# Value and gate projection of a gated linear recurrence: high and low weight parts as one 512-column product, and the output projection's first rows in two rounds

## The chip, the core and the metric

The kernel runs on one core of a Trainium2 chip. A core has a matrix engine (TensorE, written PE in the profile; its weight loads are the row PEld), a vector engine (VectorE, DVE), an engine for pointwise functions (ScalarE, ACT), a general one (GpSimd, POOL) and SyncE (SP), whose queue issues nearly all of this kernel's transfers. Each engine works through its own list of instructions in order and waits on semaphores that the other engines raise. PE reads its operands from the on-chip memory SBUF and writes only to the accumulator memory PSUM, which ACT and DVE read. The metric is the device time of the core in microseconds (us), before against after.

## The reference, cut to what matters

The model is a trunk of two layers over 1024 tokens of width 1024. The first layer mixes tokens with a gated linear recurrence in 8 heads of 128 columns, the second with windowed attention; each mixer is followed by a layer norm, a gated feed-forward with a short convolution (the ConvFFN), and another layer norm. The change lies in the first mixer:

```python
q, f, i, g = jnp.split(h @ w_in, 4, axis=-1)
fg = lb + (1.0 - lb) * jax.nn.sigmoid(heads(f))
o = hgrn2_chunkwise(jax.nn.silu(heads(q)), 1.0 - fg, heads(i), jnp.log(fg))
o = o * lax.rsqrt(jnp.mean(jnp.square(o), -1, keepdims=True) + RMS_EPS)
o = o * g_norm_w.astype(jnp.float32) * jax.nn.silu(heads(g))
return o.reshape(B, S, D).astype(h.dtype) @ w_out
```

Here `i` are the values (V in the kernel) and `silu(g)` is the output gate (G). The state of a head is a 128 x 128 matrix that decays with `fg` and takes in a key times a value at every token. All of it is float32.

## The kernel before, in words

**Three products for one.** Each float32 operand is split into a high part (a rounded copy in the type fp32r, made by ACT) and a low part (the remainder, a subtraction on DVE in `low_part`, L169). A product is then hi x hi + hi x lo + lo x hi, three matmuls that accumulate in the same PSUM columns: lines L194, L195 and L196 of `mm3`. `T[:, 0]` and `T[:, 1]` hold the high and low parts of the transposed activations, `HL` those of the weights.

**Stages of the first mixer.** For each head h the order is: `qf` projects forget gate and query (weights stationary, 512 tokens moving, four products of 24 matmuls), then `ig_block` is called four times, for pairs tp of token blocks, and projects value and gate: the 128 x 128 activations of one token block are stationary and 256 weight columns move, 128 of the value and 128 of the gate. A pair of blocks fills one PSUM tile `psmm` of 512 columns. There are four tiles `psmm`, used in turn by everything that is projected. From each, ACT takes the sigmoid of the gate (L706) and copies the value (L707), and DVE multiplies the gate by its sigmoid (L709); after that the tile is free. The very first pair of head 0 is projected by `first_rows` (L688) in an order of its own, while the input is still arriving.

**The recurrence.** `recur` of head h runs between the matmuls of the projections that follow. It is a chain over engines: DVE scales keys and queries level by level (`update`), ACT makes copies (`stash`), PE multiplies small blocks (`scores`, `blocks`), and so on to the products kd x V (L1020) and the output (L1034, L1036). Then `norm` squares on ACT, scales on DVE (L1055), and PE transposes (L1060). For head 7 the transposed output is split straight into `T` (L225, L226); the other heads' outputs wait in `Y`, and `moves` splits them into `T` later, in head 7, two token blocks at a time.

**What sets the order.** Within the first mixer the order of all engines but the transfers' landing is written out by hand with the help of a planner, the class `Order`: `od.t` is planned PE time, moved on by the cost of each matmul; `od.v` is planned DVE time; `od.tick()` after a product lets chains step whose time has come, and `lay` fills DVE with waiting work: low parts of weights (`lowparts`), low parts of moved activations (`movelows`), and block differences of the feed-forward's weights (`pending`, L1134), which have nothing to do with this layer. `slot_begin` and `slot_end` bracket each product or pair of blocks; at `slot_begin` all low parts of the slot before, and all waiting gate multiplications (`soon`), are given out at once. Past the first mixer only PE's order is written out, and the other engines' order comes from a scheduler.

**The output projection.** Its first six row blocks are begun with seven of eight contraction blocks (`out_part`), since head 7's output comes last: blocks 0 to 3 in `psmm`, 4 and 5 in the halves of a tile `psax`. `out_proj` then adds the eighth, loads the residual into `Y` (L305) and the second half of the weights (`out_late`, by way of L164), and the layer norm follows.

Of the kernel before, what the change touches and what calls it, by code (L numbers as in the profile page):

```python
# [16 lines left out]
P = 128  # L17
# [90 lines left out]
def trunk(ctx: ExitStack, tc: tile.TileContext, a: dict, out: bass.AP):  # L108
# [31 lines left out]
    def psmm():  # L140
        return mmp.tile([P, 512], F32, name="psmm")
# [57 lines left out]
    def mm32(ps, lhsT, rhs, start=True, stop=True, cost=0.218, **kw):  # L199
        nc.tensor.matmul(ps, lhsT, rhs, start=start, stop=stop, **kw)  # L200
        od.t += cost
# [451 lines left out]
    with tc.tile_pool(name="t", bufs=1, reuse_waits="tile") as raws, hgrn_pool as hp:  # L653
# [27 lines left out]
        def first_rows(us, ps, ahead):  # L681

            for i in range(2):
                passes = [(0, 0, 0), (1, 0, 0), (0, 0, 1), (1, 0, 1), (0, 1, 0), (0, 1, 1)] if i == 0 else [
                    (0, 0, 0), (0, 0, 1), (0, 1, 0), (0, 1, 1), (1, 0, 0), (1, 0, 1)]
                for n, (x, w, u) in enumerate(passes):
# [6 lines left out]
                    od.tick()  # L693

        def ig_block(h, us, tp, soon=None, ahead=None):
            if tp == 0:
                VG[h] = (hp.tile([P, NB, P], F32, name="V", bufs=2), hp.tile([P, NB, P], F32, name="G", bufs=2))
            V, G = VG[h]
            ps = psmm()
# [4 lines left out]
            pv = ps.rearrange("p (t g c) -> p t g c", t=2, g=2)  # L704
            ts = slice(2 * tp, 2 * tp + 2)
            nc.scalar.activation(G[:, ts, :], pv[:, :, 1, :], AF.Sigmoid)  # L706
            nc.scalar.copy(V[:, ts, :], pv[:, :, 0, :])  # L707
            def gate():
                nc.vector.tensor_tensor(G[:, ts, :], G[:, ts, :], pv[:, :, 1, :], op=ALU.mult)  # L709
                od.vec(0.4)  # L710

            if soon is None:
                gate()
            else:
                soon.append(od.later(1.2, gate))

# [11 lines left out]
        with tc.tile_pool(name="ep", bufs=1, reuse_waits="tile") as ep:  # L728
# [22 lines left out]
            with tc.manual_schedule(engines={EN.PE, EN.SP, EN.Activation, EN.DVE}):  # L751
# [52 lines left out]
                for tp in range(1, NB // 2 - 1):  # L804
                    ahead = od.spawn(x_pair(2 * tp + 2), 2.0)
                    ig_block(0, us, tp)
                    od.finish([ahead])
                w0["f"] = qf_split(raws0["f"])
                ig_block(0, us, NB // 2 - 1)
                w0["q"] = qf_split(raws0["q"])  # L810
                nc.vector.tensor_copy(msk, mf)

# [61 lines left out]
        def recur(h, qs, fg, kp):  # L874
# [82 lines left out]
            od.vec(4.4)  # L957
            idle = [t.rearrange("p c d -> p (c d)") for t in VG[h - 1]]
            r1 = idle[1][:, :S // 2]
            nc.vector.tensor_tensor(r1, kp[:, 0::2], qp[:, 1::2], op=ALU.mult)  # L960
# [6 lines left out]
            update(1)  # L967
            early = stash(2, idle[0])
            yield od.behind(0.0, 0.5)
# [44 lines left out]
            while values_in[0] < h:  # L1014
                yield 0.2
            V, G = VG[h]
            ps = psax()
# [57 lines left out]
        slot_no = [-1]  # L1075
        pending, soon, lowparts, movelows = [], [], [], []

# [67 lines left out]
        values_in, values_done, normed = [0], [-1], []  # L1145
        wo = a["hgrn_w_out"][0]
# [7 lines left out]
        with tc.manual_schedule(engines={EN.PE, EN.SP, EN.Activation, EN.DVE, EN.Pool}):  # L1154
# [23 lines left out]
            for h in range(1, NH):  # L1178
# [18 lines left out]
                for tp in range(NB // 2):  # L1197
                    if tp == lead[h]:
                        ready.append((h, w["out"]))
                    slot_begin()  # L1200
                    if h == NH - 1 and tp:
                        moved.append(od.spawn(moves(tp - 1), 0.8))
                        if tp == 1:
                            oraw.append(load(out_loads(rows1, 0, (6, 7))))
                    ig_block(h, us, tp, soon)
                    slot_end(2.0, *make_w[tp])
                values_in[0] = h
                if ready:
# [4 lines left out]
            while lowparts:  # L1213
                lay_low()
            od.finish([params] + moved[:2] + soon)
# [346 lines left out]
```

## Time and profile before

| | us |
|---|---|
| median of 3 runs (lowest, highest) | 2152.23 (2151.32, 2153.89) |
| the profiled execution: its own time | 2151.58 |
| its span, from first to last instruction | 2149.8 |
| PE busy | 2135.9 (99%) |
| DVE busy | 1743.3 (81%) |
| ACT busy | 918.5 (43%) |
| POOL busy | 122.1 (6%) |

The page of the profile gives busy time by engine, the span in 40 slices, the transfers, the chain of work that ended last, and the costliest groups of instructions. Other views give the same trace as stretches of time, as waits, or as a list in order of time. A row of a group reads: line, engine, operation, output<-input, shapes, count | busy time, mean nanoseconds of one | idle time before it and who ended it. Matmuls overlap in the pipeline: the duration of one (0.39 us for 512 columns) is longer than the distance from one start to the next, and only that distance is what a matmul costs PE.

### The profile page before, as it was taken

How to read it: one execution, taken by the hardware profiler on the slowest of the kernel's cores; microseconds unless marked ns; L12 is line 12 of the kernel's file. 1: busy time of each engine (PE TensorE's matmuls, PEld its weight loads, DVE VectorE, ACT ScalarE, POOL GpSimd, SP SyncE). 2: the span in 40 equal slices, each digit the busy share in tenths (PEclk: the TensorE clock that was granted, in tenths of full speed). 3: DMA queues.
4: the chain of work that ended last, by engine and by line, in shares of the span. 5: the costliest groups of instructions: out<-in, count | busy, mean ns of one | idle time of the engine just before them, and what ended most of it. 6: DMA issues, size and time to landing. Idle time of an engine off the chain costs nothing.

```text
span 2149.8 us, 33060 instructions
## 1 busy us (share of the span) xinstructions
PE 2135.9 (99%) x13165; PEld 1809.0 (84%) x13165; DVE 1743.3 (81%) x2318; ACT 918.5 (43%) x1472; POOL 122.1 (6%) x143
## 2 busy tenths in 40 slices
PE   9999999999999999999999999999999999999998
PEld 9899999898888888888888888878888888888887
DVE  3877765577999999887978558969999899878986
ACT  3344434353444444434433256743544444444430
POOL 1000000001100000000001123311000000000002
PEclk9999999999999999999999999999999999999999
DMA  5755541123222222228854411133233222249662
GB/s 200 292 204 211 177 138 41 34 85 123 99 85 95 86 89 81 82 93 284 279 186 157 128 30 30 33 118 108 89 98 98 85 82 89 79 144 329 226 213 92
DMA packets 229842, 279.03 MB, mean 130 GB/s; under 512 B 29960, under 2 KB 158648, under 8 KB 226872
## 3 DMA queue, kind: packets, MB, share of 16 engines
q1 hardware_dynamic: 228736, 276.53, 38.5%
q8 instruction: 103, 1.69, 0.3%
q10 hardware_dynamic: 856, 0.37, 0.1%
q14 instruction: 51, 0.42, 0.1%
q0 software_dynamic: 96, 0.02, 0.0%
HBM read 213.94 MB, written 62.94 MB: 129 GB/s over the span
## 4 chain that ended last, share of the span: by engine, by line
PE 96%; DVE 2%; DMA 1%; issue 0%; ACT 0%; SPq 0%; DVEq 0%; ACTq 0%
PE psmm L194 20%; PE psmm L196 20%; PE psmm L195 20%; PE psax L194 9%; PE psax L196 9%; PE psax L195 9%; PE psax L200 3%; PE psmm L204 1%; PE psmm L200 1%; PE psax L204 1%; PE psax L1356 1%; DMA rx<-in_ffn_w_out_dram 1%; DVE T L169 0%; DVE Y L473 0%; PE psmm L688 0%
## 5 line engine op out<-in xcount | busy, mean ns | idle before, releaser
L194 PE MATMUL psmm<-T,HL 128*128 128x512 f32 x768 | 305.0, 397 | 0.0
L196 PE MATMUL psmm<-T,HL 128*128 128x512 f32 x768 | 299.4, 390 | 0.0
L195 PE MATMUL psmm<-T,HL 128*128 128x512 f32 x768 | 299.1, 389 | 0.0
L473 DVE SCALAR_TENSOR_TENSOR Y<-Y,cwt 128x1023 f32<-128x1023 f32 (+1 forms) x176 | 225.1, 1281 | 41.1 <-ACT Y L471 39.5
L221 ACT CAST HL<-rx 128x1024 fp32r<-128x1024 f32 (+1 forms) x151 | 152.0, 1009 | 200.8 <-PE psmm L195 46.9
L194 PE MATMUL psmm<-HL,T 128*128 128x256 f32 (+1 forms) x640 | 192.3, 300 | 0.9 <-issue 0.9
L196 PE MATMUL psmm<-HL,T 128*128 128x256 f32 (+1 forms) x640 | 189.8, 297 | 0.0
L195 PE MATMUL psmm<-HL,T 128*128 128x256 f32 (+1 forms) x640 | 189.6, 296 | 0.0
L169 DVE TENSOR_TENSOR HL<-rx,HL 128x1024 fp32r<-128x1024 f32 (+1 forms) x151 | 174.6, 1162 | 11.0 <-ACT HL L221 10.7
L196 PEld LDWEIGHTS psmm<-T,HL 128*128 128x128 f32 x768 | 144.1, 188 | 30.9
L194 PEld LDWEIGHTS psmm<-T,HL 128*128 128x128 f32 x768 | 144.3, 188 | 28.6
L195 PEld LDWEIGHTS psmm<-T,HL 128*128 128x128 f32 x768 | 144.4, 188 | 27.9
L471 ACT ACTIVATE Y<-Y,cwt 128x1024 f32<-128x1024 f32 x88 | 109.0, 1239 | 99.3 <-DVE Y L460 90.5
L194 PE MATMUL psax<-T,HL 128*128 128x512 f32 x352 | 137.3, 390 | 0.0
L196 PE MATMUL psax<-T,HL 128*128 128x512 f32 x352 | 137.0, 389 | 0.0
L195 PE MATMUL psax<-T,HL 128*128 128x512 f32 x352 | 137.0, 389 | 0.0
L195 PEld LDWEIGHTS psmm<-HL,T 128*128 128x128 f32 x640 | 122.3, 191 | 4.2 <-issue 1.0
L243 POOL TENSOR_TENSOR rs<-rs,nhalf 128x1 f32<-128x1 f32 x32 | 46.2, 1445 | 1398.7 <-DVE rs L242 1398.7
L194 PEld LDWEIGHTS psmm<-HL,T 128*128 128x128 f32 x640 | 122.3, 191 | 3.7 <-issue 0.4
L196 PEld LDWEIGHTS psmm<-HL,T 128*128 128x128 f32 x640 | 122.2, 191 | 3.5 <-DVE T L169 0.3
L169 DVE TENSOR_TENSOR HL<-raw,HL 128x1024 fp32r<-128x1024 f32 x51 | 62.2, 1222 | 71.9 <-ACT HL L176 71.8
L221 ACT CAST HT<-rx 128x1024 fp32r<-128x1024 f32 (+1 forms) x37 | 35.6, 962 | 113.9 <-DVE rx L427 74.3
(302 smaller groups left out, 5117.7 us busy)
## 6 DMA issues: line engine op xcount, KB each, us to landing
rx<-in_ffn_w_in_dram SPq DMA_DIRECT2D x136, 256.0 KB, 3.1
rx<-gd SPq DMA_DIRECT2D x118, 256.0 KB, 3.8
Y<-in_ffn_w_out_dram SPq DMA_DIRECT2D x44, 512.0 KB, 5.7
bsd<-Y SPq DMA_DIRECT2D x22, 1024.0 KB, 5.2
gd<-Y SPq DMA_DIRECT2D x44, 512.0 KB, 2.6
rx<-in_ffn_w_out_dram SPq DMA_DIRECT2D x54, 256.0 KB, 4.3
R<-bsd SPq DMA_DIRECT2D x44, 256.0 KB, 5.0
Y<-in_ffn_w_in_dram SPq DMA_DIRECT2D x40, 256.0 KB, 3.1
```

Source lines behind the costliest of these rows:

```text
L169: make = lambda e: e.tensor_tensor(lo, src, hi.bitcast(F32), op=ALU.subtract)
L194: nc.tensor.matmul(ps, st(0), mv(0), start=start, stop=False)
L195: nc.tensor.matmul(ps, st(0), mv(1), start=False, stop=False)
L196: nc.tensor.matmul(ps, st(1), mv(0), start=False, stop=stop)
L200: nc.tensor.matmul(ps, lhsT, rhs, start=start, stop=stop, **kw)
L204: nc.tensor.transpose(ps, src, ident)
L221: nc.scalar.copy(hi, src)
L243: nc.gpsimd.tensor_tensor(rs, rs, nhalf, op=ALU.pow)
L471: nc.scalar.activation(c, u, AF.Identity, bias=cwt[:, l, 3, ci:ci + 1], scale=cwt[:, l, 2, ci:ci + 1])
L473: nc.vector.scalar_tensor_tensor(c[:, sh:], u[:, :S - sh], cwt[:, l, 2 - sh, ci:ci + 1], c[:, sh:], op0=ALU.mult, op1=ALU.add)
L1356: nc.tensor.matmul(pv[:, e, jj, lo:], q[bp // 2][es, e, qs], Kl[es, pp, ks] if low else Kh[:, pp, e, ks], start=not low and jj == 0, stop= ...
```

## The change

**Value and gate.** For every token block but the first two of head 0, the three matmuls of 256 columns become two. The first has the high part of the activations stationary and moves the high and the low part of the weights behind each other, 512 columns, into a whole tile `psmm`: columns 0 to 255 receive hi x hi, columns 256 to 511 receive hi x lo. The second has the low part of the activations stationary and adds lo x hi to the first 256 columns. The two halves still have to be added, so the new chain `values` takes the place of the sigmoid, copy and multiplication that read PSUM: ACT copies the right half to SBUF, DVE adds the left half, and after each second block ACT takes the sigmoid of the gates and DVE multiplies. Each token block now takes a tile `psmm` of its own. `V` and `G` become one tile `VG` with value and gate beside each other.

**Planner.** A contraction block of this projection is now booked with 0.347 us of planned PE time; it was 3 x 256 / 2365 = 0.325. Low parts and chains left over from one slot are given out at the end of the next slot (`rest`), not at its beginning.

**Output projection.** Blocks 0 to 3 are begun in two rounds: first all products of the high activations with both weight parts, for the four blocks, then the products of the low activations for the four blocks. The low parts of moved activations are asked for only ahead of the second round.

```diff
-        VG = {-1: tuple(hp.tile([P, NB, P], F32, name=n, bufs=2) for n in "VG")}
+        VG = {-1: hp.tile([P, NB, 2, P], F32, name="VG", bufs=2)}
+        def values(h, tb, ps):
+            vg = VG[h][:, tb]
+            nc.scalar.copy(vg, ps[:, 256:].rearrange("p (g c) -> p g c", g=2))
+            yield 0.9
+            nc.vector.tensor_tensor(vg, vg, ps[:, :256].rearrange("p (g c) -> p g c", g=2), op=ALU.add)
+            od.vec(0.45)
+            if tb == NB - 1:
+                values_in[0] = h
+            if tb % 2:
+                G = VG[h][:, tb - 1:tb + 1, 1, :]
+                sg = hp.tile([P, 2, P], F32, name="sg")
+                yield 0.7
+                nc.scalar.activation(sg, G, AF.Sigmoid)
+                yield 0.8
+                nc.vector.tensor_tensor(G, G, sg, op=ALU.mult)
+                od.vec(0.4)
...
+            for tb in () if ahead else (2 * tp, 2 * tp + 1):
+                ps, ts = psmm(), slice(tb * P, (tb + 1) * P)
+                for kc in range(KC):
+                    w = us[kc // 4]
+                    nc.tensor.matmul(ps, T[:, 0, kc, ts], w[:, :, kc % 4, :], start=kc == 0, stop=False)
+                    nc.tensor.matmul(ps[:, :256], T[:, 1, kc, ts], w[:, 0, kc % 4, :], start=False, stop=kc == KC - 1)
+                    od.t += 0.347
+                    od.tick()
+                soon.append(od.spawn(values(h, tb, ps)))
...
-            if ahead:
-                first_rows(us, ps, ahead)
-            else:
-                proj_tok(us, tp, ps)
-            nc.scalar.activation(G[:, ts, :], pv[:, :, 1, :], AF.Sigmoid)
-            nc.scalar.copy(V[:, ts, :], pv[:, :, 0, :])
-            def gate():
-                nc.vector.tensor_tensor(G[:, ts, :], G[:, ts, :], pv[:, :, 1, :], op=ALU.mult)
-                od.vec(0.4)
...
+            od.finish(gated[h])
             og = hp.tile([P, NB, P], F32, name="og")
...
-        def slot_begin():
+        def rest():
             while lowparts:
                 lay_low()
-            od.finish(soon)
-            soon.clear()
+            od.finish(old)
+            soon[:] = [t for t in soon if t[1] is not None]
+            old[:] = soon
...
         def slot_end(wait, *makes):
+            rest()
...
             for tb in range(4):
                 begun.append(psmm())
+                ts = slice(tb * P, (tb + 1) * P)
+                for w in range(2):
+                    for kc in range(KC - 1):
+                        nc.tensor.matmul(begun[tb], T[:, 0, kc, ts], us[kc][:, w, :], start=w + kc == 0, stop=False)
+                        od.t += 512 / 2365.0
+                        od.tick()
+            for tb in range(4):
+                ts = slice(tb * P, (tb + 1) * P)
                 movelows.sort(key=lambda m: m[0])
                 while movelows and movelows[0][0] <= tb // 2:
                     lay_moved()
-                out_part(begun[tb], us, tb, range(KC - 1))
+                for kc in range(KC - 1):
+                    nc.tensor.matmul(begun[tb], T[:, 1, kc, ts], us[kc][:, 0, :], start=False, stop=False)
+                    od.t += 512 / 2365.0
+                    od.tick()
```

More of the change, by code (lines that the diff above doesn't have):

```diff
@@ L669, in qf_split @@
             return split_raw(raw, eng).rearrange("p h (k c) -> p h k c", k=KC)
-        VG = {-1: tuple(hp.tile([P, NB, P], F32, name=n, bufs=2) for n in "VG")}
+        VG = {-1: hp.tile([P, NB, 2, P], F32, name="VG", bufs=2)}
+        values_in, soon, gated = [-1], [], {}
+        def values(h, tb, ps):
[14 more added lines that the diff above has]
+                od.vec(0.4)
@@ new lines, in first_values, with ig_block @@
+        def first_values(ps):
+            pv = ps.rearrange("p (t g c) -> p t g c", t=2, g=2)
+            vg = VG[0][:, :2]
+            nc.scalar.activation(vg[:, :, 1, :], pv[:, :, 1, :], AF.Sigmoid)
+            nc.scalar.copy(vg[:, :, 0, :], pv[:, :, 0, :])
+            yield 1.4
+            nc.vector.tensor_tensor(vg[:, :, 1, :], vg[:, :, 1, :], pv[:, :, 1, :], op=ALU.mult)
+            od.vec(0.4)
+        def ig_block(h, us, tp, ahead=None):
+            if tp == 0:
+                VG[h] = hp.tile([P, NB, 2, P], F32, name="VG", bufs=2)
+            if ahead:
+                ps = psmm()
+                first_rows(us, ps, ahead)
+                soon.append(od.spawn(first_values(ps)))
+                gated[h] = soon[-1:]
+            for tb in () if ahead else (2 * tp, 2 * tp + 1):
[7 more added lines that the diff above has]
+                soon.append(od.spawn(values(h, tb, ps)))
+                gated.setdefault(h, []).append(soon[-1])
+                od.tick()
@@ L673, in ig_first, with soon_all @@
+        def soon_all(left=0):
+            while len(soon) > left:
+                od.finish([soon.pop(0)])
         def ig_first(raw):
@@ L693, in first_rows @@
                     od.tick()
[L695 to L699, printed above, removed]
-            if ahead:
-                first_rows(us, ps, ahead)
-            else:
-                proj_tok(us, tp, ps)
[L704 to L707, printed above, removed]
-            def gate():
-                nc.vector.tensor_tensor(G[:, ts, :], G[:, ts, :], pv[:, :, 1, :], op=ALU.mult)
-                od.vec(0.4)
[L712 to L715, printed above, removed]
         still = Y[:, 7, :P]
@@ L807, in trunk @@
                     od.finish([ahead])
+                    soon_all(1)
                 w0["f"] = qf_split(raws0["f"])
@@ L957, in recur @@
             od.vec(4.4)
-            idle = [t.rearrange("p c d -> p (c d)") for t in VG[h - 1]]
-            r1 = idle[1][:, :S // 2]
+            idle = VG[h - 1].rearrange("p c g d -> p (c g d)")
+            r1 = idle[:, S:S + S // 2]
             nc.vector.tensor_tensor(r1, kp[:, 0::2], qp[:, 1::2], op=ALU.mult)
@@ L967, in recur @@
             update(1)
-            early = stash(2, idle[0])
+            early = stash(2, idle[:, :S])
             yield od.behind(0.0, 0.5)
@@ L1075, in trunk @@
         slot_no = [-1]
-        pending, soon, lowparts, movelows = [], [], [], []
+        pending, lowparts, movelows, old = [], [], [], []
         def lay_low():
@@ L1203, in trunk @@
                         if tp == 1:
+                            rest()
                             oraw.append(load(out_loads(rows1, 0, (6, 7))))
-                    ig_block(h, us, tp, soon)
+                    ig_block(h, us, tp)
                     slot_end(2.0, *make_w[tp])
-                values_in[0] = h
                 if ready:
@@ L1214, in trunk @@
                 lay_low()
-            od.finish([params] + moved[:2] + soon)
+            soon_all()
+            od.finish([params] + moved[:2])
             moved.append(od.spawn(moves(NB // 2 - 1), 3.0))
```

7 lines of the change are left out of this document (5 added, 2 removed).

## The prediction

> **What bounds the kernel now.** I read the page first, then the engines by stretch, PE's waits, and lists in order of time.
>
> ```profile
> span 2149.8 us, 33060 instructions
> PE 2135.9 (99%) x13165; PEld 1809.0 (84%) x13165; DVE 1743.3 (81%) x2318; ACT 918.5 (43%) x1472; POOL 122.1 (6%) x143
> PEclk9999999999999999999999999999999999999999
> PE 96%; DVE 2%; DMA 1%; issue 0%; ACT 0%; SPq 0%; DVEq 0%; ACTq 0%
> ```
>
> PE is busy 99% of the span at full granted clock, and 96% of the chain that ended last is PE. A busy PE need not be at its peak, so the question is what a matmul costs it and whether it stands still where the change is made: the first mixer, up to 500 us. By stretch (columns: us; PE, PEld, DVE, ACT, POOL busy; clock; DMA share, GB/s), and PE's longest waits before and after 500 us:
>
> ```profile
> 37.00:500.00 463.00, 462.14 (x4982) 414.94 (x4981) 300.68 (x521) 191.94 (x417) 17.00 (x16) 1.00 0.42 149
> 531.00:700.00 169.00, 168.19 (x774) 139.54 (x773) 164.35 (x211) 78.19 (x100) 9.29 (x7) 1.00 0.28 94
> PE psmm L194 <- issue: 0.9, 1, 0.9
> PE psmm L196 <- DVE HL L169: 1.6, 2, 0.8
> ```
>
> PE idles 0.86 us in 463, DVE a third of it. So here time is the sum of PE's starts-to-starts, and every other engine has room. Only the feed-forward behind it (531 to 700 us) has DVE at 97%, with one PE wait of 0.8 us for a low part per layer (1.6 in two).
>
> **Part 1: three matmuls become two.** Start to start is what counts:
>
> ```profile
> 59.80 0.39 PE L194 MATMUL psmm<-T,HL 128*128 128x512 f32 x1
> ...
> 65.92 0.39 PE L194 MATMUL psmm<-T,HL 128*128 128x512 f32 x1
> 84.56 0.39 PE L196 MATMUL psmm<-T,HL 128*128 128x512 f32 x1
> 84.79 0.28 PE L194 MATMUL psmm<-HL,T 128*128 128x256 f32 x1
> 86.86 0.28 PE L194 MATMUL psmm<-HL,T 128*128 128x256 f32 x1
> ...
> 91.42 0.28 PE L196 MATMUL psmm<-HL,T 128*128 128x256 f32 x1
> L194 PE MATMUL psmm<-HL,T 128*128 128x256 f32 x560 | 160.3, 286 | 0.9 <-issue 0.9
> ```
>
> From 59.80 to 65.92 lie 27 starts: 0.2267 us per 512 columns. From 86.86 to 91.42 lie 38: 0.1200 us per 256. Twice 0.1200 less 0.2267 is 13.3 ns: what one more instruction costs PE beyond its columns. A 512 followed by a 256 (84.56 to 84.79) costs its own 0.23, so alternating them should add nothing. Old: 3 x 0.1200 = 0.3600 per contraction block; new: 0.2267 + 0.1200 = 0.3467. Of the 560 on L194, 64 are the shared value projection of the second layer (4 pairs x 2 blocks x 8) and stay; 496 change (8 heads x 8 blocks x 8, less the 16 of the first pair). 496 x 13.3 ns = 6.6 us off PE: 0.64 in head 0, 0.85 in each other head. This stays as long as nothing else ends later than PE.
>
> The Trainium skill ("TensorE: Matmul & The Clock Gate", section "Back-to-back issue gap") gives N/2.4 + 2.5 ns as the isolated warm gap. By it the extra instruction would cost 2.5 ns, and the sum would be an estimated 1.2 us instead of 6.6. The trace's gaps are 11 ns longer at both widths, so I go by the trace.
>
> The two weight halves moved in one instruction lie apart in SBUF. No row shows a 512-column read in two pieces. Bounds: nothing, and 13.3 ns each (a second piece as dear as a second instruction, which cancels the gain). I take nothing, since columns are streamed at the same rate in both widths above.
>
> **Part 2: more reading of PSUM.** The nearest rows:
>
> ```profile
> L709 DVE TENSOR_TENSOR G<-G,psmm 128x256 f32<-128x256 f32 x32 | 13.3, 416 | 23.9 <-ACT V L707 23.9
> L706 ACT ACTIVATE G<-psmm 128x256 f32<-128x256 f32 x32 | 12.2, 383 | 59.8 <-PE psmm L196 59.8
> L707 ACT COPY V<-psmm 128x256 f32<-128x256 f32 x32 | 11.8, 369 | 0.0
> L169 DVE TENSOR_TENSOR HL<-raw,HL 128x1024 fp32r<-128x1024 f32 x51 | 62.2, 1222 | 71.9 <-ACT HL L176 71.8
> L955 DVE TENSOR_TENSOR St<-qs,kp 128x1024 f32<-128x1024 f32 x8 | 9.8, 1219 | 0.0
> L964 DVE TENSOR_TENSOR kd<-kp,qp 128x512 f32<-128x512 f32 x16 | 10.3, 685 | 0.0
> 447.64 0.28 PE L196 MATMUL psmm<-HL,T 128*128 128x256 f32 x1
> 450.21 0.38 ACT L706 ACTIVATE G<-psmm 128x256 f32<-128x256 f32 x1
> 452.97 0.41 DVE L709 TENSOR_TENSOR G<-G,psmm 128x256 f32<-128x256 f32 x1
> ```
>
> 62 additions of L709's form: 62 x 0.416 = 25.8 us more DVE; 62 copies for 31: 31 x 0.369 = 11.4 us more ACT. DVE's 300.7 of 463 becomes 326 of 457, 71%: covered, on average. Against it, DVE stood 71.9 us before low parts of weights whose high part ACT had not made yet, because they were given out right after the cast; now they come a slot later, and most of that standing should go.
>
> The cover is thin at one point: the tiles `psmm`. A pair used to hold one tile and had three pairs (17 us) to give it back; now a block holds one and has three blocks, 3 x 8 x 0.3467 = 8.3 us. In the rows above PE issued a pair's last matmul at 447.64 and its gate was multiplied at 452.97: a lag of 5.5 us to its end at 453.38. The worst queue ahead of an addition is the head's opening burst (two of L955's size, six of half: 6.5 us by their 1.22 and 0.69, end to end). DVE takes that burst as soon as its inputs stand, mostly before the block ends; I therefore take no wait.
>
> **Part 3: head 7.** Its chain is the tightest:
>
> ```profile
> 466.81 1.65 ACT L1002 COPY A<-Ab 32x256 f32<-32x256 f32 x4
> 468.47 0.39 ACT L706 ACTIVATE G<-psmm 128x256 f32<-128x256 f32 x1
> 469.14 1.05 ACT L221 CAST T<-Y 128x1024 fp32r<-128x1024 f32 x1
> 470.57 1.01 ACT L1012 COPY kd<-psax 128x1024 f32<-128x1024 f32 x1
> 468.39 1.09 PE L204 MATMUL psax<-ident,kp 128*128 128x128 f32 x8
> 472.07 1.16 PE L200 MATMUL psax<-V,kd 128*128 128x128 f32 x9
> ```
>
> kd is ready at 471.58, its user starts at 472.07: 0.5 us of slack. In the new order the last block's copy, the addition on DVE (0.42) and the sigmoid stand in this ACT queue ahead of the same cast: 0.5 us more than L706 and L707 took. Two gate chains (0.42 each, with a sigmoid of 0.38 between) stand ahead of the DVE updates that feed it: up to 0.6 more. And PE arrives one 512 matmul earlier (11 instead of 12 between the transposes of 468.39 and it): 0.23. That is 1.3 against 0.5: a wait of up to 0.8 us; I take 0.7. In heads 0 to 6 the casts of `T` are not there, and the numbers of matmuls between steps stay within one or two of what they were; none to 0.7 each.
>
> **Part 4: output projection in two rounds.** 56 matmuls and 28 of 512 columns are the same 84: no PE time. The moved low parts go to DVE later, the last two behind head 7's product with the gate (L1039). SP's queue waits for these: the residual loads of `Y`, and behind them the second weight half.
>
> ```profile
> 473.61 5.23 SPq L305 DMA_DIRECT2D Y<-in_x_dram  x7
> 480.63 1.23 DVE L1039 TENSOR_TENSOR og<-psax,G 128x1024 f32<-128x1024 f32 x1 [3.34 <-PE psax L200]
> 486.00:488.00 2.00, 2.00 (x11) 1.65 (x10) 0.84 (x1) 0.00 (x0) 1.12 (x1) 1.00 1.04 392
> 488.00:490.00 2.00, 2.00 (x10) 1.66 (x9) 0.38 (x1) 0.00 (x0) 0.00 (x0) 1.00 0.24 92
> 497.95 2.94 ACT L221 CAST TX<-rx 128x1024 fp32r<-128x1024 f32 x3
> ```
>
> Released at 473.6, ten transfers of 512 KB were in by 488.7, 15.1 us later, and were first used at 497.95: 9.2 us of slack. The new release is after L1039 and one low part, 481.86 + 1.22 = 483.1 on the old clock, so the last lands at 498.2: just when ACT comes for the first. I take nothing; if the casts slip, PE's next tile waits behind them, 0 to 2 us.
>
> **Part 5: the feed-forward.** PE's order past this point is unchanged, but DVE's and ACT's order in the first layer's feed-forward differs for some 260 DVE instructions, same set. The one PE wait there, 0.8 us, can go or grow by a couple of half-size operations: -0.8 to +2. I take 0.
>
> **Sum.** -6.6 + 0.7 = -5.9 on the profiled execution's 2151.58: 2145.7. The median lies 0.65 above that execution, so 2146.3 as a median. With every bound at its best: -7.4, 2144.8. With 0.7 in each of seven heads, 2 at the transfers and 2 in the feed-forward: +2.3, 2154.5.
>
> **Rivals.**
> *Tiles not given back (slower).* If an addition stands behind the burst, one scaled output (1.22), two low parts (2.4) and its own copy and 0.42, a tile comes back 0.37 + 6.5 + 1.22 + 2.4 + 0.42 = 10.9 us after its block: PE waits 2.6, in one block of each of seven heads 18: 18 - 6.6 = +11.6, 2163.8. It decides from 8.3 us of lag; more than 10.9 us must be lost in all to end slower by 0.2%. For it: the 5.5 us lag shown. Against: the third of idle DVE. 13%, feed-forward and transfer mishaps of that size with it.
> *Waits eat part of it.* 0.3 to 1.5 us in each head as in head 7, since ACT and DVE now wait for each other twice per pair: 2 to 10 us, ending within 0.2%, say 2150. 15%.
> *It does not do what it says.* The 13.3 ns do not go with the instruction: the read in two pieces, or the wider product itself, costs them again. Gain 0, head 7's 0.7 stays: 2152.9. 5%, since a 512 followed by a 256 shows no such cost. The page's gap rule above would land near this rival, an estimated 1.2 us lower.
>
> **How the numbers follow.** My forecast has 67%: 2144.8 to 2147.9 alone. 0.2% is 4.3 us, about what a measurement of this kernel can tell from no change; faster than 2147.9 is 67%, within it 20% (second and third rival), slower 13%. The range 2144.0 to 2153.0 leaves out most of the first rival and little else.
>
> **What would show it.** Right: 512 and 256 alternate at 0.347 us a pair; L688's first pair is unchanged; the kd product of head 7 has a wait under 1 us on ACT; the output projection starts about 6 us earlier; idle of L169 on raw weights falls well below 72. Wrong: PE waits on `psmm` released by the addition on DVE, pairs dearer than 0.36, a late cast of TX, or new PE waits between 531 and 750 us.

## The result, and the profile after

The changed kernel takes 2148.18 us (median of 15 runs, 2147.51 to 2149.81) against 2152.23 (15 runs beside it). The ratio is 0.9982, 95% interval 0.9975 to 0.9988: 4.05 us or 0.18% less. That lies in the predicted range and on the side that was predicted. But it is two thirds of the 5.9 us forecast, just outside the 2144.8 to 2147.9 us to which the prediction gave 67%, and just inside what it called "within 0.2%". The profiled execution has a span of 2146.1 us, 3.7 less than before.

From the page of the changed kernel, its engines by stretch (us; PE, PEld, DVE, ACT, POOL busy; clock; DMA share, GB/s) and PE's waits:

```profile
span 2146.1 us, 32133 instructions
...
PE 2130.6 (99%) x12669; PEld 1780.8 (83%) x12669; DVE 1764.6 (82%) x2380; ACT 930.8 (43%) x1503; POOL 119.4 (6%) x143
```
```profile
37.00:494.00 457.00, 454.88 (x4514) 387.34 (x4513) 319.13 (x578) 202.32 (x443) 14.97 (x16) 1.00 0.43 151
528.00:697.00 169.00, 169.00 (x779) 140.44 (x777) 164.84 (x211) 78.85 (x102) 9.55 (x7) 1.00 0.28 94
```
```profile
PE psmm L1263 <- DVE HL L169: 1.2, 1, 1.2
...
PE psmm L196 <- DVE HL L169: 1.0, 1, 1.0
...
PE psax L200 <- issue: 1.0, 1, 1.0
```

PE has 496 instructions fewer and 5.3 us less busy time. DVE does 18 us more in the first mixer and is at 70% there. In the first mixer PE now idles 2.1 us instead of 0.9, and the new piece is a 1.2 us wait of the output projection (L1263) for a low part of weights. From 528 to 697 us its idle time is gone.

Where the time goes is read at marks that both kernels have: one set of eight transposes in the start-up (called the start below), the St sums of head 7, its kp transposes, the first transposes of the feed-forward, the first transposes of the second layer. Their rows, in the kernel before and in the changed one:

```profile
20.80 1.04 PE L204 MATMUL psax<-ident,Y 128*128 128x128 f32 x8
...
453.97 0.64 PE L200 MATMUL psax<-St,one 128*32 128x256 f32 x8
...
531.03 1.03 PE L204 MATMUL psmm<-ident,Y 128*128 128x128 f32 x8
...
1167.94 1.03 PE L204 MATMUL psax<-ident,Y 128*128 128x128 f32 x8
```
```profile
20.46 1.03 PE L204 MATMUL psax<-ident,Y 128*128 128x128 f32 x8
...
450.05 0.64 PE L200 MATMUL psax<-St,one 128*32 128x256 f32 x8
...
465.45 1.09 PE L204 MATMUL psax<-ident,kp 128*128 128x128 f32 x8
...
528.09 1.03 PE L204 MATMUL psmm<-ident,Y 128*128 128x128 f32 x8
...
1163.38 1.03 PE L204 MATMUL psax<-ident,Y 128*128 128x128 f32 x8
```

At the start the changed kernel is 0.34 us ahead, at the St sums 3.92. At head 7's kp transposes (468.39 before) it is 2.94: about 1 us went to the new wait. It stays 2.94 to the feed-forward, becomes 4.56 through the first feed-forward, and ends at 3.7. A second profile of the same changed kernel (below) gives 0.92, 4.42, 3.44, 3.41, 4.46 and 4.2, so half a microsecond of each number need not be the change.

### The profile page after: what moved, and what is told of

The parts are those of the page before. It is cut to its first block, busy times and chain, and to the rows that moved or that the text cites. A ratio compares the mean times of both kernels' runs of the same rounds, so it can differ in the third digit from the quotient of the medians.

```text
span 2146.1 us, 32133 instructions
## 1 busy us (share of the span) xinstructions
PE 2130.6 (99%) x12669; PEld 1780.8 (83%) x12669; DVE 1764.6 (82%) x2380; ACT 930.8 (43%) x1503; POOL 119.4 (6%) x143
## 3 DMA queue, kind: packets, MB, share of 16 engines
q8 instruction: 99, 1.62, 0.3%
## 4 chain that ended last, share of the span: by engine, by line
PE 95%; DVE 3%; DMA 2%; issue 1%; ACT 0%; SPq 0%; DVEq 0%; ACTq 0%
PE psmm L194 17%; PE psmm L196 17%; PE psmm L195 16%; PE psax L194 9%; PE psax L195 9%; PE psax L196 9%; PE psmm L714 5%; PE psax L200 3%; PE psmm L715 3%; PE psmm L204 2%; PE psmm L200 1%; PE psax L1406 1%; PE psax L204 1%; DVE Y L473 1%; DVE T L169 1%
## 5 line engine op out<-in xcount | busy, mean ns | idle before, releaser
L714 PE MATMUL psmm<-HL,T 128*128 128x512 f32 x496 | 176.9, 399 | 0.0
L715 PE MATMUL psmm<-HL,T 128*128 128x256 f32 x496 | 138.9, 280 | 0.0
L714 PEld LDWEIGHTS psmm<-HL,T 128*128 128x128 f32 x496 | 93.1, 188 | 21.1
L715 PEld LDWEIGHTS psmm<-HL,T 128*128 128x128 f32 x496 | 93.7, 189 | 0.4
L169 DVE TENSOR_TENSOR HL<-raw,HL 128x1024 fp32r<-128x1024 f32 x51 | 62.6, 1228 | 19.9 <-ACT HL L176 19.7
L196 PEld LDWEIGHTS psax<-T,HL 128*128 128x128 f32 x352 | 66.0, 188 | 13.7
L194 PEld LDWEIGHTS psax<-T,HL 128*128 128x128 f32 x352 | 66.1, 188 | 13.7
```

Of the source, the lines that this page charges most:

```text
L169: make = lambda e: e.tensor_tensor(lo, src, hi.bitcast(F32), op=ALU.subtract)
L194: nc.tensor.matmul(ps, st(0), mv(0), start=start, stop=False)
L196: nc.tensor.matmul(ps, st(1), mv(0), start=False, stop=stop)
L714: nc.tensor.matmul(ps, T[:, 0, kc, ts], w[:, :, kc % 4, :], start=kc == 0, stop=False)
L715: nc.tensor.matmul(ps[:, :256], T[:, 1, kc, ts], w[:, 0, kc % 4, :], start=False, stop=kc == KC - 1)
```

## The experiments

Each is an edit of the changed kernel unless it says otherwise. "The span" is that of the profiled execution: 2149.8 before, 2146.1 changed.

### What a pair of products costs

The pairs (L714 with 512 columns, L715 with 256) do not have one pace. In the changed kernel's timeline:

```profile
30.70 0.39 PE L714 MATMUL psmm<-HL,T 128*128 128x512 f32 x1
...
37.77 0.40 PE L714 MATMUL psmm<-HL,T 128*128 128x512 f32 x1
...
103.16 0.40 PE L714 MATMUL psmm<-HL,T 128*128 128x512 f32 x1
...
110.09 0.40 PE L714 MATMUL psmm<-HL,T 128*128 128x512 f32 x1
```

Between the first two rows lie 20 pairs: 0.3535 us each. Between the last two lie 20 as well: 0.3465. Every unbroken stretch keeps one of the two paces; of the 476 pairs in stretches long enough to tell, about 275 are dear and 201 cheap, and the mean over the stretches is 0.3504. (Only the first pair of a stretch is longer, 0.43 us behind most breaks. With these, and up to the start of what PE does next, all 496 pairs take 176.0 us.) Three explanations were put to the chip: the read of weights in two pieces, the change of width from instruction to instruction, and what PE did just before the stretch.

**Weights side by side.**

```diff
-            return split_raw(raw, eng).rearrange("p h (k c) -> p h k c", k=4)
...
+            hl = hl_at(...).rearrange("p a n -> p (a n)").rearrange("p (k h c) -> p h k c", k=4, h=2)
+            return split_into(hl, raw.rearrange("p (k c) -> p k c", k=4), eng)
...
```

> Edit: in the changed kernel the high and the low part of a value/gate weight unit are laid out side by side (256 high columns, then their 256 low columns), so that the 512 columns of one product are one contiguous read; nothing else moves. In the changed kernel's profile some 201 pairs take 0.3467 us and some 275 take 0.3533. Theory 1, the read in two pieces costs the 6.6 ns: all pairs take 0.3467, 275 x 6.6 ns = 1.8 us less, span 2146.1 - 1.8 = 2144.3. Theory 2, the alternation of widths costs it, and theory 3, it hangs on what PE did just before the stretch: both kinds of stretches stay where they are, span 2146.1 within 0.4.

Measured: 2148.46 us, ratio 0.998 (0.9971 to 0.9989), span 2147.4. Of the long stretches only two, both in the start-up, went over to 0.3469; all others kept their pace to 0.002. In the second profile of the unedited changed kernel one stretch at 86 us went over too, from 0.3533 to 0.3467, with nothing edited. So the two-piece read, which the prediction took at nothing, costs nothing that shows, and the 1.8 us did not come. The span is 1.3 us above the 2146.1 of theories 2 and 3; at the first transposes of the feed-forward this kernel is still 0.2 us ahead of the changed one, so the difference arises behind the value products, and this profile is the slowest of the run's eleven executions.

**The 512s first, then the 256s.**

```diff
-                for kc in range(KC):
-                    nc.tensor.matmul(ps, T[:, 0, kc, ts], w[:, :, kc % 4, :], ...)
-                    nc.tensor.matmul(ps[:, :256], T[:, 1, kc, ts], w[:, 0, kc % 4, :], ...)
...
+                for kc in range(KC):
+                    nc.tensor.matmul(ps, T[:, 0, kc, ts], us[kc // 4][:, :, kc % 4, :], ...)
...
+                for kc in range(KC):
+                    nc.tensor.matmul(ps[:, :256], T[:, 1, kc, ts], us[kc // 4][:, 0, kc % 4, :], ...)
```

> Edit: in the changed kernel the eight products of 512 columns of a block of tokens come first, then its eight of 256 columns, instead of by turns; the weights' layout stays in two pieces. Theory 2, the alternation costs the 6.6 ns: gaps of 0.2267 and 0.1200 throughout, eight pairs in 2.773 us everywhere, 1.8 us less, span 2144.3. Theory 1, the read in two pieces costs it: the gaps of the 512s are 0.233 somewhere and the sum stays, span 2146.1 within 0.4. Theory 3, the phase left by the work before the stretch: some stretches stay dearer, others not, span 2145 to 2146.1.

Measured: 2148.91 us, ratio 0.9983 (0.9974 to 0.9992), span 2146.4. From its timeline:

```profile
104.30 2.00 PE L713 MATMUL psmm<-HL,T 128*128 128x512 f32 x8
106.14 1.11 PE L717 MATMUL psmm<-HL,T 128*128 128x256 f32 x8
107.09 2.00 PE L713 MATMUL psmm<-HL,T 128*128 128x512 f32 x8
```

Eight and eight take 2.79 us, 0.349 a pair, in the whole blocks of the timeline. The two paces are gone, but the pace that took their place is nearly their mean: all pairs together take 175.7 us, against 176.0, where theory 2 had 1.8 less. The rows show why: eight 512s take 1.84 us where eight times 0.2267 is 1.81, and eight 256s 0.95 where eight times 0.1200 is 0.96. In this order the two changes of width of a block cost about 0.02 us, while the cheap stretches of the changed kernel change width at every product and pay nothing.

**Every second pair turned round.**

```diff
...
+                    pair = (low, both) if kc % 2 else (both, low)
...
```

> Edit: in the changed kernel every second pair is turned round (512, 256, 256, 512, 512, 256 and so on), so that widths change half as often; same products, same sums. In the changed kernel a pair takes 0.3467 us in some stretches and 0.3533 in others, whether the two weight halves lie apart or side by side; in blocks of eight 512s and eight 256s it took 0.349. Theory 2, each change of width may cost time: pairs between 0.3467 and 0.350 everywhere, span 2144.6 to 2145.5. Theory 3, what PE did just before a stretch sets its pace for the whole stretch: two kinds of stretches again, 6 ns apart, span 2146.1 within 0.8.

Measured: 2146.86 us, ratio 0.9972 (0.9962 to 0.9983), span 2146.3. Stretches that were dear became shorter (the one from 205 us 11.93 instead of 12.09), those that were cheap longer (the one from 154 us 16.80 instead of 16.73); together 175.3 instead of 176.0. That is theory 2's band for the pace, but the span gained nothing. At the first transposes of the feed-forward this kernel is 0.46 us ahead of the changed one; it loses 0.83 up to the second layer, where PE waits twice for `Y` (0.47 and 0.32 us, L326 and L594) and the changed kernel's profile not at all. This profile is also the slowest of the run's eight executions.

What the three show: strictly by turns a pair costs 0.3467 or 0.3533, either other order tried costs about 0.348 to 0.349, and the layout made no difference but in two stretches of the start-up. That the pace changes only where other work breaks a stretch fits theory 3; what in that work sets it stays open.

**Three products again, all else as changed.** This undoes part 1 alone.

```diff
-                    nc.tensor.matmul(ps, T[:, 0, kc, ts], w[:, :, kc % 4, :], ...)
+                    nc.tensor.matmul(ps[:, :256], T[:, 0, kc, ts], w[:, 0, kc % 4, :], ...)
+                    nc.tensor.matmul(ps[:, 256:], T[:, 0, kc, ts], w[:, 1, kc % 4, :], ...)
                     nc.tensor.matmul(ps[:, :256], T[:, 1, kc, ts], w[:, 0, kc % 4, :], ...)
```

> Edit: the changed kernel with each pair of products (512 and 256 columns) made by three of 256 again, into the same tile, and all else as it is (addition, sigmoid, order of low parts, two rounds). 496 more matmuls. Theory A, the fewer instructions are the whole gain: 496 x (0.3600 - 0.3505, the mean of the pairs) = 4.7 us more, span 2150.8, about the kernel before. The prediction's size, 13.3 ns each, would be 6.6 us, span 2152.7. Theory B, the later low parts and the changed order earned part of it: less than 3 us more, span under 2149.

Measured: 2150.86 us, ratio 0.9993 (0.9984 to 1.0002), span 2148.5.

```profile
103.51 0.28 PE L714 MATMUL psmm<-HL,T 128*128 128x256 f32 x1
...
110.71 0.28 PE L714 MATMUL psmm<-HL,T 128*128 128x256 f32 x1
...
465.93 1.43 PE L1264 MATMUL psmm<-HL,T 128*128 128x512 f32 x5 [1.06 <-DVE HL L169]
```

Twenty triples take 7.20 us, 0.3600 each, and this pace is the same in every long stretch. Against 0.3504 the 496 pairs save 9.6 ns each, 4.8 us; added up as above, the triples take 180.6 us against 176.0, 4.6 more. In the heads most of it is there: from the start to the St sums of head 7 this kernel loses 0.45 us on the kernel before, where the changed one wins 3.58, so the pairs are worth 4.0 us there. But by the numbers that were expected theory B holds: 2.4 us more of span, 2.7 by the medians. This kernel is 1.3 us of span below the kernel before, and 1.1 us of that comes between the first transposes of the feed-forward and the second layer. So a part of the gain is not the products'. Why the spans differ by 2.4 and not by 4 is seen: this profile was 1.2 us ahead of the changed kernel's at the start, and from the second layer on the changed kernel's profile loses 0.9 us on the kernel before and this one none. Whether the same makes up the 2.7 of the medians stays open.

The last row shows one thing more. The wait of the output projection for a weight's low part is there too (1.06 us, against 1.16), although PE comes to head 7's St sums 2.84 us later than in the changed kernel. So this wait goes with the companion edits, not with the instructions saved.

### What the companions of the products are worth

**One round in the output projection.**

```diff
-                for w in range(2):
-                    for kc in range(KC - 1):
-                        nc.tensor.matmul(begun[tb], T[:, 0, kc, ts], us[kc][:, w, :], ...)
...
-                for kc in range(KC - 1):
-                    nc.tensor.matmul(begun[tb], T[:, 1, kc, ts], us[kc][:, 0, :], ...)
...
+                out_part(begun[tb], us, tb, range(KC - 1))
```

> Edit: the changed kernel with the output projection's first four row blocks in one round again (three products per contraction block, moved low parts laid out block by block), all else as it is. Read at two marks: the first transposes of the feed-forward (531.0 before, 528.1 in the changed kernel) and the end (span 2146.1). Theory A, the two rounds are what made the last output weight's low part late (first used at the 14th product instead of the 20th), and what turned the order in the first feed-forward: the 1.16 us wait shrinks to a few tenths, the first mark comes at about 527, the feed-forward's low-part wait of 0.8 us comes back and the second mark is at 2146.1 within 0.5. Theory B, as predicted the two rounds cost and bring nothing in the first mixer: the first mark stays at 528.1 within 0.3.

Measured: 2153.83 us, ratio 1.0007 (0.9998 to 1.0016), span 2151.7. Theory A has the feed-forward right (a low-part wait there is back, 1.7 us), but the first mark came at 531.4, where the theories had 527 and 528. Its PE and DVE timelines:

```profile
460.86 0.39 PE L195 MATMUL psmm<-HL,T 128*128 128x512 f32 x1
465.15 0.50 PE L196 MATMUL psmm<-HL,T 128*128 128x512 f32 x1 [3.91 <-DVE T L169]
```
```profile
460.99 1.22 DVE L169 TENSOR_TENSOR HL<-raw,HL 128x1024 fp32r<-128x1024 f32 x1
462.90 0.42 DVE L679 TENSOR_TENSOR VG<-VG,psmm 128x256 f32<-128x256 f32 x1 [0.69 <-ACT VG L677]
463.80 0.42 DVE L689 TENSOR_TENSOR VG<-VG,sg 128x256 f32<-128x256 f32 x1 [0.48 <-ACT sg L687]
464.15 4.09 DVE L169 TENSOR_TENSOR T<-Y,T 128x768 fp32r<-128x768 f32 x4
```

In one round the 15th product already reads the moved low part of `T` (kc 4 to 6). DVE makes it behind a weight's low part and the last block's addition and gate; PE stands 3.9 us. The kernel before needs the same operand at the same place and does not wait:

```profile
463.31 0.98 DVE L169 TENSOR_TENSOR T<-Y,T 128x768 fp32r<-128x768 f32 x1
```
```profile
466.37 0.39 PE L196 MATMUL psmm<-HL,T 128*128 128x512 f32 x1
```

There it was ready 2.1 us ahead (464.29 against 466.37). With the pairs PE comes there 5.3 us sooner (460.86 and 0.23 for the 14th product is 461.09), and DVE takes the operand later in its queue. The two rounds make its first use the 61st product instead of the 15th, and the wait is gone.

**Low parts at the beginning of a stage.**

```diff
         def slot_begin():
+            rest()
...
         def slot_end(wait, *makes):
-            rest()
```

> Edit: the changed kernel with waiting low parts (and the earlier value chains) given out at the beginning of the next stage again instead of at its end, all else as it is. DVE's standing before low parts of raw weights should go back from 14.8 to some 70 us. Theory A, that standing is covered (DVE 70% busy) and the earlier low part frees the output projection: PE's 1.16 us wait goes, no new one comes, span about 2145. Theory B, with an addition per block the standing now holds up additions and so the tiles psmm: PE waits on psmm released by DVE, 1 to 8 us in all, span 2146 to 2153.

Measured: 2151.76 us, ratio 0.9997 (0.9988 to 1.0005), span 2149.9: theory B's span, but mostly by other waits than the one that it names. In this kernel's groups (37 to 494 us) and PE timeline:

```profile
L169 DVE TENSOR_TENSOR HL<-raw,HL 128x1024 fp32r<-128x1024 f32 x33 | 40.3, 1225 | 57.5 <-ACT HL L176 57.5
```
```profile
169.06 0.47 PE L714 MATMUL psmm<-HL,T 128*128 128x512 f32 x1 [0.90 <-DVE VG L679]
...
454.63 0.74 PE L200 MATMUL psax<-qp,kp 128*32 128x16 f32 x64 [1.38 <-DVE kp L979]
...
461.86 0.70 PE L200 MATMUL psax<-qp,kp 128*32 128x32 f32 x32 [0.70 <-DVE kp L979]
...
472.46 1.83 PE L200 MATMUL psax<-VG,kd 128*128 128x128 f32 x14 [1.02 <-ACT kd L1045]
```

DVE stands 57.5 us before raw weights (13.3 in the changed kernel in that stretch, 66.6 before). In the kernel before that cost PE nothing; here it does: one tile `psmm` comes back 0.9 us late, and head 7's updates and kd are late three times, 3.1 us in all.

**The products alone.** Both companions undone at once.

> Edit: the changed kernel with both companions of the products undone: one round in the output projection, and low parts given out at the beginning of a stage. What is left of the change is the two products with their additions. Undone singly, the rounds cost 5.6 us and the place of the low parts 3.8 us of span. Theory A, the two losses are separate (one for moved low parts in the output projection, one for DVE standing before raw weights all through the heads): they add, span about 2146.1 + 9.4 = 2155.5, slower than before. Theory B, both are the one backlog of DVE in head 7: about the larger, span 2151.5 to 2153.

Measured: 2159.66 us, ratio 1.0032 (1.002 to 1.0045), span 2158.8: slower than before. The losses add, and more (9.4 expected, 12.7 of span measured). PE's waits and the row of the largest:

```profile
PE psmm L196 <- DVE T L169: 5.5, 1, 5.5
PE psmm L196 <- DVE HL L169: 2.6, 2, 1.4
PE psax L200 <- DVE kp L979: 2.1, 2, 1.4
PE psax L194 <- DVE Y L594: 1.4, 2, 0.9
```
```profile
471.04 0.80 PE L196 MATMUL psmm<-HL,T 128*128 128x512 f32 x1 [5.49 <-DVE T L169]
...
474.89 1.87 PE L204 MATMUL psax<-ident,kp 128*128 128x128 f32 x8
```

At the end of the heads it was 2.97 us ahead of the kernel before (451.00 against 453.97); at the kp transposes it is 6.50 behind (474.89 against 468.39). So 9.5 us are lost in some 24 us of head 7, and by the end another 2.5.

**The two rounds alone, in the kernel before.**

> Edit: the kernel before with the output projection's two rounds alone; value and gate products, low parts and tiles as before. Undone in the changed kernel, the two rounds cost 5.6 us, 3.9 of it one wait of PE for a moved low part. Theory A, they bring nothing of their own and only cover what DVE is behind in head 7 by parts 1 and 2: in the kernel before PE waits for no moved low part, so the first transposes of the feed-forward stay at 531.0 within 0.3 and the span at 2149.8 within 1. Theory B, they gain by themselves, through the order they give the first feed-forward: that mark stays, and the span falls by 1 to 1.6 us.

Measured: 2150.57 us, ratio 0.9991 (0.9982 to 1.0), span 2148.7. The first mixer is unchanged (St sums at 453.55, feed-forward at 530.61: 0.42 earlier in both; 0.32 of it is there at the start). The second layer begins at 1166.35, 1.59 earlier, so 1.2 us come in the first feed-forward, whose order of work on DVE and ACT differs with the rounds though PE's does not. There is one low-part wait of 1.1 us in this kernel instead of two of 0.8. So the first mixer goes as theory A says, and the span, 1.1 us less, as theory B says. By the medians the gain is 1.4 us, at the edge of what the interval can tell from none.

**Additions 2.1 us later.**

```diff
             nc.scalar.copy(vg, ps[:, 256:].rearrange("p (g c) -> p g c", g=2))
-            yield 0.9
+            yield 3.0
```

> Edit: the changed kernel with each block's addition on DVE given out 3.0 us behind its copy instead of 0.9 (the sigmoid and the gate's product 2.1 us later with it). It probes the cover of the tiles psmm, 8.3 us by the prediction. Theory A, the lag stays under 8.3 us: no PE wait on psmm released by DVE, span 2146.1 within 0.5. Theory B, the cover is thinner than that: PE waits before the first product of a block in several heads, 0.3 to 1 us each, span 2148 to 2152.

Measured: 2152.22 us, ratio 0.9994 (0.9985 to 1.0003), span 2151.3. No wait on `psmm` released by the addition, as theory A says, and yet 5 us more span. The largest wait is again L1263 for a weight's low part, 2.0 us instead of 1.2, and the first feed-forward gains nothing on the kernel before (0.85 behind it at its beginning, 0.82 at its end). From the St sums to the kp transposes it loses 2.1 us on the changed kernel: 0.85 of it is that wait, and the 32 products `kd` just ahead of the transposes take 1.92 us instead of 1.09. The tiles' cover holds; head 7's operands come late. (By the ratios to the kernel before the loss is smaller, 2.6 us.)

### A better version

**Head 7's waiting low parts before its last pair of blocks.**

```diff
                         if tp == 1:
                             rest()
                             oraw.append(load(out_loads(rows1, 0, (6, 7))))
+                        if tp == 3:
+                            rest()
```

> Edit: in the changed kernel's head 7 the waiting low parts of output weights are given out before the last pair of value blocks, as in the kernel before, instead of behind it. Theory A, the one low part that DVE made at 461.81 is all that PE's 1.16 us wait in the output projection's first round hangs on, and time behind it follows: that wait is gone, span 2146.1 - 1.2 = 2144.9. Theory B, the next link is as late: DVE stands about 1 us for ACT's cast of that unit ahead of head 7's updates, kd is ready later while PE comes 1.2 us earlier, and PE waits 0.5 to 1.2 us before the kd product instead: span 2145.4 to 2146.1.

Measured: 2146.80 us, ratio 0.9976 (0.9966 to 0.9985), span 2144.7. The wait at L1263 is gone. The next links show, but small:

```profile
458.68 0.70 PE L200 MATMUL psax<-qp,kp 128*32 128x32 f32 x32 [0.26 <-DVE kp L979]
459.30 4.80 PE L1265 MATMUL psmm<-HL,T 128*128 128x512 f32 x20
...
468.83 1.83 PE L200 MATMUL psax<-VG,kd 128*128 128x128 f32 x14 [0.16 <-ACT kd L1045]
```

From the St sums to the kp transposes the changed kernel loses 0.98 us on the kernel before, this one 0.41: half of the wait came through, and the two small ones took most of the rest, as theory B has it. At the feed-forward it is 0.42 us ahead of the changed kernel's first profile and level with its second. The rest of the 1.4 us of span comes in the feed-forwards, so theory A's 2144.9 was met by another way than the one it gives. The 1.4 us of the medians are less than the two intervals can tell apart.

**That and every second pair turned round**, beside a second profile of the changed kernel on the same chip.

> Edit: the changed kernel with head 7's waiting low parts given out before its last pair of blocks, and every second pair of products turned round. Alone the first gave a span of 2144.7 (1.4 less), the second took 0.7 us off the value stretches. Theory A, the two add: span about 2144.0, pairs at a mean of 0.349, no wait in the output projection's first round. Theory B, PE 0.7 us earlier meets head 7's kd and the feed-forward's low part 0.7 us too early, and waits: span 2144.5 to 2145.5.

> The changed kernel itself, beside the three above: how far its span and its start (the eight transposes at 20.5 us) move from one profile to the next. Two profiles of one kernel should agree within 0.3%: span 2146.1 within 1, pairs at 0.3467 and 0.3533 in the same stretches, the 1.16 us wait in the output projection there again.

Measured: the combination 2145.67 us, ratio 0.9968 (0.9956 to 0.9981), span 2143.7; the changed kernel again 2148.53, ratio 0.9982 (0.9973 to 0.9991), span 2145.6. The two gains add (theory A), with one wait of 0.3 us for kp left in head 7. This version beats both kernels: 6.3 us below the kernel before in that comparison (2151.93), 2.9 below the changed one (2145.03 to 2147.49 against 2146.16 to 2149.45, on the same chip). The second profile shows what a single one is worth: its start came 0.92 us earlier than in the kernel before instead of 0.34, and the feed-forward's wait on `Y` (L594) was at 1034.78 instead of 1981.77.

## Why the prediction was right, and where it was not

The direction and the mechanism of the main term were right; the sum was too good by a third, and how much of it hung on the two companion edits was not seen. By its own steps:

**Part 1** (6.6 us) was mis-sized: it is the term that failed. 0.3600 a triple holds, but the pair was put at 0.2267 + 0.1200 = 0.3467 with "alternating them should add nothing". The stretches show 0.3504 on average, so the saving is 9.6 ns an instruction, 4.8 us (4.6 added up directly), of which 4.0 reached the end of the heads. The one-row proof (a 512 to a 256 at 0.23) was too short: the 6.6 ns of a dear pair are below what rows rounded to 10 ns show in one gap. The truth lies between the two prices that the text weighed. By the Trainium skill ("TensorE: Matmul & The Clock Gate", section "Back-to-back issue gap"), whose formula for the isolated warm gap adds 2.5 ns an instruction, the saving would have been an estimated 1.2 us; the runs do not bear that out. By the plain rows it was 13.3 ns an instruction, and 9.6 came. The two-piece read was rightly taken at nothing, as far as the run with the weights side by side can show.

**Part 2** was right in its numbers and in what it excluded. The groups of the changed kernel:

```profile
L169 DVE TENSOR_TENSOR HL<-raw,HL 128x1024 fp32r<-128x1024 f32 x51 | 62.6, 1228 | 19.9 <-ACT HL L176 19.7
...
L679 DVE TENSOR_TENSOR VG<-VG,psmm 128x256 f32<-128x256 f32 x62 | 25.7, 417 | 12.8 <-ACT VG L677 12.8
```

25.7 us of additions against 25.8, DVE at 70% against 71%, the standing before raw weights 19.9 instead of 71.9, and no wait of PE on a tile that an addition gives back. But "covered, on average" hid where the cover is thin. It named the tiles `psmm`; the thin place is the moved and weight low parts of head 7, which the output projection reads at once.

**Part 3** (0.7 us) did not come: kd was copied at 466.64 for 1.02 us, and its product began at 468.91. But this is because PE had lost 1.16 us just before; with that wait mended, 0.16 us of it appears.

**Part 4** ("no PE time", 0) is right for the rounds alone in the kernel before, and right on the transfers: residual loads at 479.63 instead of 473.61, the casts of `TX` at 493.64 (497.95 before), no wait of PE. It is wrong in the changed kernel, both ways. It missed that a low part given out a stage later is needed sooner, since the first round reads all low weights within a block's first 14 products:

```profile
458.68 3.25 PE L1263 MATMUL psmm<-HL,T 128*128 128x512 f32 x13
463.08 1.42 PE L1263 MATMUL psmm<-HL,T 128*128 128x512 f32 x5 [1.16 <-DVE HL L169]
```
```profile
461.81 1.22 DVE L169 TENSOR_TENSOR HL<-raw,HL 128x1024 fp32r<-128x1024 f32 x1
```

And it missed that without the rounds PE would stand 3.9 us for a low part of `T`: the step costed at nothing was worth 5.6 us of span.

**Part 5** (0, bounds -0.8 to +2) was on the wrong side by more than its bound: the first feed-forward gave 1.6 us (1.1 in the second profile). The prediction counted one PE wait there, but the kernel before has two, and the changed kernel's first profile has neither; its second keeps 0.41 us of the wait for `Y`. What the first has instead is a wait for `Y` in the second layer. The two rows of the kernel before, then one of the changed kernel:

```profile
629.52 0.50 PE L196 MATMUL psmm<-TX,HL 128*128 128x512 f32 x1 [0.81 <-DVE HL L169]
...
1039.29 0.50 PE L194 MATMUL psax<-HT 128*128 128x512 f32 x1 [0.56 <-DVE Y L594]
```
```profile
1981.77 0.50 PE L194 MATMUL psax<-HT 128*128 128x512 f32 x1 [0.47 <-DVE Y L594]
```

From the second layer on the changed kernel lost 0.9 us in one profile and 0.3 in the other. The rounds alone, in the kernel before, give 1.2 us in the first feed-forward, but the other kernels with two rounds gave between 0.0 (additions later) and 2.1 us (512s first, or the low parts of the better version) there. So this term moves with any change of order ahead of it, and it is not shown to belong to the rounds.

Together, on the profile: 4.03 + 0.34 - 0.45 - 0.98 + 1.62 - 0.87 = 3.69 us. These are part 1, the start, all else in the heads, head 7 up to its kp transposes (the low part), the first feed-forward, and all from the second layer on. That the sum came so near owes something to luck: the feed-forward that was put at nothing gave back more than the wait that was not seen had taken.

**The rivals.** "Tiles not given back" did not happen; its mechanism shows once, 0.9 us, when low parts are given out as before. A slower ending was near all the same, by another way: without its two companions the change is 7.7 us slower than the kernel before by the medians. "Waits eat part of it" came true in one head, not in each. "It does not do what it says" is refuted for the instruction, and half true for its price.

## What to carry to other kernels

A matmul saved makes PE arrive earlier everywhere behind it, and work moved in another engine's list makes operands come later. List the operands that are made just in time for the next stage (here the low parts of head 7) and compare their slack with both before calling the other engines covered: with DVE 70% busy on average, one operand was still 3.9 us late. A reordering that costs no instruction can be the part that pays: work out what each companion edit costs not only against the kernel before but also with the main edit in place. A pace taken from one pair of rows should be checked over twenty of them, in several stretches.

## What the hardware showed that was not expected

Strictly alternating products of 512 and 256 columns run at one of two steady paces, 0.3467 or 0.3533 us a pair, at full granted clock, with nothing waited for, and hold it until other work breaks the stretch. Twenty triples of 256 columns in the same places ran at 0.3600 throughout. In nearly all stretches the pace is the same from one profile to the next and across layouts; what fixes it was not found.
